# Twenty-three units of weights multiplied as plain fp32 in a two-block model of 2816- and 1280-wide layers

## The chip, the cores and the metric

One core of one Trainium2 chip runs the whole program in one launch. The metric is device time in microseconds from the first to the last instruction of the core; the median of the runs counts. Engines are named as in the profile: PE (TensorE) multiplies, PEld is its weight load, DVE is VectorE, ACT is ScalarE, POOL is GpSimd, SP is SyncE, whose queue issues the transfers of the weights.

## The reference

A block of two layers on 256 tokens of 1024 features, then a second block of two layers on those tokens and 16 meta tokens, 272 in all. Everything is float32.

```
x = layer_norm(ALPHA*x + 0.5*swiglu(x, w_in, w_out))          # 22 tiles of 128 wide
mix = (gelu(y_br) * rg_lru(conv(u_br), gate_w, ...)) @ w_out  # first layer: 1280 wide
mix = dilated_attention(x, k, v, w_q, w_o)                    # second layer
proj = h @ w_in                                               # second block, twice:
mix = concat(retention, pooling, forgetting attention) @ w_out
h = layer_norm_2(ALPHA*h + mix); h = layer_norm_2(ALPHA*h + (silu(h@w1) * (h@w3)) @ w2)
```

In `rg_lru` two gates are products of the convolved `u` with 256x256 blocks of `gate_w`, five blocks for each gate; from the gates come the factors of a scan along the tokens.

## The kernel before

**Tiling.** Activations stand with the features on the partitions: `xf[:, k, tokens]` is feature tile k of 8 in fp32. Every product of weights is a row of multiplies with a 128x128 weight tile as the stationary operand and 256 or 272 token columns as the moving one, summed over k in a PSUM bank.

**Splitting.** A number x is written as a high part (x rounded to fp32r) and a low part (x minus the high part). A weight tile is multiplied three times as fp32r (`mm3`): high by high, high by low, low by high. The activations are split into `gh` and `gl` by the norms, the convolved `u` into `uch` and `ucl`, the recurrent stage's output into `yh` and `yl`.

**Weights.** All weights come in one stream of 537 units of 8 tiles (128x1024, 512 KB), in the order in which PE uses them. `_dma` fetches unit u into one of 5 buffers `raw`, on SP's queue. `_hi` makes `whi` of it in two ACT casts of 128x512 (L87), `_lo` makes `wlo` in two subtractions (L99) on DVE, or on POOL while `lo_pool` is set. A buffer `raw` is free again when its `wlo` is made. `pump` runs ahead of PE by up to 6 units, and `w` hands out the tiles.

**Stages around the change.** `rg` is the recurrent stage, units 66 to 100. Its first 4 output tiles (`filler`) are multiplied before the norm is finished, the statistics of the norm lie amid them. Then: 4 tiles of `u` (units 70 to 73), gates 0 (74), 2 tiles of `u` (75, 76), gates 1 and 2 (77, 78), and gelu groups 0 to 4 of two units each with gates 3 and 4 between them (79 to 90). DVE makes the convolutions (L508, L510), the split of `uc` (L515, L516), the scans (L561) and the gelu's polynomial (L547, L548, L550); ACT makes tanh, exp and sqrt. At last `out_proj` multiplies `yh` and `yl` (units 91 to 100) in 8 output tiles, the first four together, so that the fifth pair of rows of `y` is wanted in unit 95. While `filler` is over and `out_proj` has not begun, `lo_pool` is set: POOL makes the low parts of the units that are split in that time.

`mixer(0)` is the first mixer of the second block, from unit 347: six tiles (`emb_filler`) before two norms are finished, then with 272 columns a group of two (`G`, units 353 and 354: keys of the retention with the forget logits, and values), pairs V_F (355, 356), K_R and Q_R (357, 358), Q_R and U_P (359, 360), and further pairs with the attention's heads between them. The logits go through some 20 small DVE instructions to `cs`, which SP's queue copies into `Kz`; the first head's scores need it between units 359 and 360.

**Order.** The instructions of an engine are run in their order, and each waits for what it needs. A tile framework sets the order from the code, the priorities (`high_priority` around the norms) and its own schedule.

Of the kernel before, what the change touches and what calls it, by code (L numbers as in the profile page):

```python
# [8 lines left out]
F32 = mybir.dt.float32  # L9
# [27 lines left out]
RAWS = 5  # L37
N_HEADS = 16
# [19 lines left out]
class Builder:  # L58
# [13 lines left out]
    # ---------------------------------------------------------------- weights  # L72
# [7 lines left out]
    def _hi(self):  # L80
        u = self.nhi
        while self.ndma < min(u + RAWS, N_UNIT):
            self._dma()
        self.nhi += 1
        hi = self.p_w.tile([128, UNIT * 128], F32R, tag="whi", name="whi")
        for q in range(0, UNIT * 128, 512):
            self.nc.scalar.copy(hi[:, q:q + 512], self.raws[u][:, q:q + 512])  # L87
        self.his[u] = hi

    def _lo(self, pool=False):  # L90
# [3 lines left out]
        self.nlo += 1  # L94
        lo = self.p_w.tile([128, UNIT * 128], F32R, tag="wlo", name="wlo")
# [6 lines left out]
    def pump(self, n, pool=False):  # L102
        """Splits up to n more units of weights, the high parts one unit ahead of the low parts."""
# [7 lines left out]
    def w(self, spec, n=1):  # L111
# [3 lines left out]
        if o == 0:  # L115
            self.his.pop(u - 1, None)
            self.los.pop(u - 1, None)
            if not self.hold:
                self.pump(2)
# [3 lines left out]
        if n == 1:  # L123
            self.plan.append(spec)
        else:
            self.plan.extend(spec)
        return self.his[u][:, o * 128:(o + n) * 128], self.los[u][:, o * 128:(o + n) * 128]

    # ---------------------------------------------------------------- helpers
    def bank(self, n=1, hold=None):  # L130
        """The next free psum bank (or aligned pair, or three in a row); a held one is skipped until it is let go."""
# [17 lines left out]
    def mm3(self, out, w, xh, xl, start, stop):  # L149
# [19 lines left out]
    # ---------------------------------------------------------------- layer norm  # L169
# [4 lines left out]
    def emb_begin(self):  # L174
        """The columns and the meta tokens that the norm of all tokens adds to the first block's last one."""
# [8 lines left out]
    def sums(self, m, N, off, sq, eng, eng2=None):  # L184
        """Running sums of x and x^2 over the feature tiles."""
# [17 lines left out]
    def fold_to(self, m, ln, N):  # L203
        """Factor and columns of the next stage's first input."""
# [13 lines left out]
    def prep(self, ms, ln, N, off, fold=True):  # L218
        """What the next norm needs of the feature tiles ms, which end together."""
# [24 lines left out]
    def scale_in(self, m, ln, N, off):  # L244
        """x <- x g, once the sums have what they need of it."""
# [9 lines left out]
    def stats(self, N, eps, tail=None, dst=None):  # L255
        """Mean and deviation of every token from the running sums; tail: the last tile's share comes on top."""
# [23 lines left out]
    def table(self, func, after):  # L280
        """Has ScalarE load the table set of func ahead of its use."""
        self.nc.scalar.activation(self.dummy, after, func)

    def norm(self, ln, N, off):
        """Normalises all feature tiles, software-pipelined over VectorE and ScalarE."""
# [17 lines left out]
    def norm_last(self, ln, N, off, i, eng, rstd, nm):  # L303
        """Normalises a feature tile that scale_in has been over."""
# [17 lines left out]
    def filler(self, specs, ln, N, off, eps, pool, tag="fv", bufs=2, when=(1, 3)):  # L322
        """First output tiles of a stage, from the not yet normalised input."""
# [16 lines left out]
    def emb_filler(self, specs, eps_in, eps, pool, tag):  # L340
        """The first output tiles of the second block, from the first block's last sums: two norms are still to come.
        The first one is of the tokens without the meta tokens, the second one of all."""
# [46 lines left out]
    def group(self, specs, N, kout=False, mid=None):  # L389
        """Output tiles in pairs from the normalised input; returns one [128, 2, N] psum view per pair.  # L390
        mid: what is emitted after the first half."""
# [6 lines left out]
        for i, (k, t) in enumerate(order):  # L398
# [3 lines left out]
            self.mm3(P[t // 2][:, t % 2, :], self.w(specs[t](k)), self.gh[:, k, 0:N], self.gl[:, k, 0:N], st, k == KD - 1)  # L402
# [5 lines left out]
    def out_proj(self, K, hh, hl, spec, coef, ln, N, off, fold, waves, korder=None, hooks={}):  # L408
        """x <- x + coef * (h @ W), in waves of output tiles; hooks: what is emitted amid the first wave."""
# [22 lines left out]
    # ---------------------------------------------------------------- feed forward  # L432
# [26 lines left out]
    # ---------------------------------------------------------------- RG-LRU  # L459
    def rg(self, ln_in, ln_out, eps):  # L460
        nc = self.nc
        N, off = SEQ, META
        with self.tc.tile_pool(name="rg", bufs=1) as p:
# [38 lines left out]
            uc, uch, ucl = {}, {}, {}  # L502

            def conv(n, src):
# [8 lines left out]
                uch[n] = p.tile([128, 2, N], F32R, tag="uch", name="uch", bufs=2)  # L513
                ucl[n] = p.tile([128, 2, N], F32R, tag="ucl", name="ucl", bufs=2)
                nc.vector.tensor_copy(uch[n], c)  # L515
                nc.vector.tensor_tensor(ucl[n], c, uch[n].bitcast(F32), op=ALU.subtract)  # L516

            def gates(n):
                P = []
                for g in range(2):  # L520
                    b = self.pair_bank(N)
                    for m in range(2):
                        for k in range(2):
                            self.mm3(b[:, m, :], self.w(("rg_gate_w", (0, g, n), k, m * 128)), uch[n][:, k], ucl[n][:, k],
                                     k == 0 and m == 0, k == 1)
# [14 lines left out]
            self.lo_pool = True  # L540
# [57 lines left out]
            self.lo_pool = False  # L598
# [3 lines left out]
    # ---------------------------------------------------------------- shared keys and values  # L602
# [34 lines left out]
    # ---------------------------------------------------------------- dilated attention  # L637
    def attn(self, ln_in, ln_out, eps):
        nc = self.nc
        N, off = SEQ, META  # L640
        with self.tc.tile_pool(name="attn", bufs=1) as p:
# [20 lines left out]
            def put(pr, g, src):  # L662
                """High part of a head's queries in its own half of the partitions, low part in the other one."""
# [70 lines left out]
            def step(n=1):  # L734
                """Head i's scores while the heads before it are a stage further each."""
# [37 lines left out]
    # ---------------------------------------------------------------- second block's mixer  # L773
# [668 lines left out]
```

## Time and profile before

| | |
|---|---|
| runs | 1810.32, 1812.07, 1812.13 us; median 1812.07 us |
| span of the profiled execution | 1813.3 us, its only own time that is known |
| mean granted PE clock | 0.970 |
| PE, DVE, ACT, POOL busy | 96%, 70%, 57%, 13% |
| weight splits | 1074 casts on ACT; 1032 subtractions on DVE, 42 on POOL |

A PE that is busy in these tables is one that has a multiply under way; multiplies overlap, so the distance between the starts of two neighbours tells what one costs, and the duration of one is longer than that. A plain fp32 multiply stands in the trace as two records, an fp32r one as one.

### The profile page before, as it was taken

The numbers are of one execution on the slowest core, as the hardware profiler recorded it, in microseconds if no ns is written. First come the engines' busy times: TensorE is split into PE (matmuls) and PEld (weight loads), VectorE is DVE, ScalarE is ACT, GpSimd is POOL, SyncE is SP. The second block draws the span as 40 slices with busy tenths as digits, with TensorE's granted clock in tenths as the row PEclk, the third lists the DMA queues.
The fourth block names the chain that finished last, engine by engine and source line by source line (L and its number), as shares of the span: only waits on it lengthen the run. The fifth ranks groups of instructions, "written<-read, shape, count | busy, mean of one in ns | idle before, by whom it ended". The sixth has DMA issues, their size and how long they took to land.

```text
span 1813.3 us, 34554 instructions
## 1 busy us (share of the span) xinstructions
PE 1741.0 (96%) x13558; PEld 1675.4 (92%) x13558; DVE 1272.0 (70%) x2399; ACT 1032.6 (57%) x2090; POOL 230.0 (13%) x266
## 2 busy tenths in 40 slices
PE   8999978999999999999999999799999999999997
PEld 8999977999999999977789999788999998899996
DVE  6666899966676666756668666897965569687653
ACT  6444666744465444644547445775744457575443
POOL 0001355000100001201120001320200030120001
PEclk9999988999999999968999999999999999999999
DMA  8555435565548555732225555433365554246550
GB/s 292 185 187 186 145 105 168 170 209 186 182 156 280 186 187 186 208 118 82 82 85 179 188 183 184 154 106 106 118 208 176 177 188 152 83 129 223 186 186 35
DMA packets 85372, 296.80 MB, mean 164 GB/s; under 512 B 10892, under 2 KB 14232, under 8 KB 84696
## 3 DMA queue, kind: packets, MB, share of 16 engines
q1 hardware_dynamic: 80216, 283.79, 47.1%
q0 software_dynamic: 1424, 7.38, 1.3%
q10 hardware_dynamic: 3568, 3.41, 0.6%
q8 instruction: 106, 1.74, 0.4%
q14 instruction: 58, 0.48, 0.1%
HBM read 290.24 MB, written 4.19 MB: 162 GB/s over the span
## 4 chain that ended last, share of the span: by engine, by line
PE 82%; DVE 11%; ACT 3%; issue 2%; DMA 1%; POOL 1%; DVEq 0%; SPq 0%; POOLq 0%; ACTq 0%
PE ps L147 81%; DVE wlo L99 3%; DMA KL<-kl 1%; PE ps L155 1%; ACT whi L87 1%; DVE uc L510 0%; DVE gl L300 0%; DVE T L561 0%; DVE xf L252 0%; POOL wlo L99 0%; DVE nt L291 0%; DVE gl L215 0%; POOL acc L193 0%; DVE rstd L277 0%; DMA raw<-in_wst_dram 0%
## 5 line engine op out<-in xcount | busy, mean ns | idle before, releaser
L87 ACT CAST whi<-raw 128x512 fp32r<-128x512 f32 x1074 | 615.5, 617 | 525.7 <-issue 311.0
L99 DVE TENSOR_TENSOR wlo<-raw,whi 128x512 fp32r<-128x512 f32 x1032 | 685.7, 701 | 321.5 <-ACT whi L87 319.6
L147 PE MATMUL ps<-gh,whi 128*128 128x256 f32 (+3 forms) x2864 | 829.0, 290 | 19.6 <-ACT gh L297 8.7
L147 PE MATMUL ps<-gl,whi 128*128 128x256 f32 (+3 forms) x2864 | 823.3, 288 | 1.0 <-DVE gl L300 1.0
L147 PE MATMUL ps<-gh,wlo 128*128 128x256 f32 (+3 forms) x2864 | 818.4, 286 | 0.0
L147 PEld LDWEIGHTS ps<-gh,whi 128*128 128x128 f32 x2864 | 549.3, 192 | 27.2 <-ACT gh L297 9.3
L147 PEld LDWEIGHTS ps<-gl,whi 128*128 128x128 f32 x2864 | 550.9, 192 | 5.9 <-issue 2.6
L147 PEld LDWEIGHTS ps<-gh,wlo 128*128 128x128 f32 x2864 | 551.1, 192 | 1.3 <-issue 0.7
L147 PE MATMUL ps<-hh,wlo 128*128 128x256 f32 (+1 forms) x1056 | 298.0, 282 | 0.0
L147 PE MATMUL ps<-hh,whi 128*128 128x256 f32 (+1 forms) x1056 | 297.9, 282 | 0.0
L147 PE MATMUL ps<-hl,whi 128*128 128x256 f32 (+1 forms) x1056 | 297.7, 282 | 0.0
L147 PEld LDWEIGHTS ps<-hl,whi 128*128 128x128 f32 x1056 | 199.0, 188 | 0.0
L147 PEld LDWEIGHTS ps<-hh,whi 128*128 128x128 f32 x1056 | 199.0, 188 | 0.0
L147 PEld LDWEIGHTS ps<-hh,wlo 128*128 128x128 f32 x1056 | 198.8, 188 | 0.0
L193 POOL TENSOR_TENSOR acc<-xf 128x256 f32<-128x256 f32 (+1 forms) x10 | 7.6, 759 | 1060.7 <-DVE xf L252 907.7
L443 DVE TENSOR_TENSOR th<-th,ps 128x512 f32<-128x512 f32 (+1 forms) x62 | 42.9, 691 | 54.3 <-PE ps L147 54.3
L193 POOL TENSOR_TENSOR acc<-acc,xf 128x256 f32<-128x256 f32 (+1 forms) x50 | 45.5, 910 | 192.3 <-DVE xf L252 177.3
L99 POOL TENSOR_TENSOR wlo<-raw,whi 128x512 fp32r<-128x512 f32 x42 | 63.3, 1536 | 46.2 <-ACT whi L87 46.2
L252 DVE SCALAR_TENSOR_TENSOR xf<-ps,xf 128x256 f32<-128x256 f32 (+1 forms) x80 | 32.9, 422 | 41.1 <-PE ps L147 40.9
L198 ACT ACTIVATE sq<-xf 128x256 f32<-128x256 f32 (+1 forms) x88 | 35.6, 410 | 44.6 <-DVE xf L252 36.8
L211 ACT ACTIVATE gh<-xf,prm 128x256 fp32r<-128x256 f32 (+1 forms) x64 | 32.1, 508 | 47.9 <-DVE xf L252 47.9
L215 DVE SCALAR_TENSOR_TENSOR gl<-xf,prm,gh 128x256 fp32r<-128x256 f32 (+1 forms) x64 | 44.5, 706 | 11.0 <-ACT gh L211 11.0
(330 smaller groups left out, 1927.8 us busy)
## 6 DMA issues: line engine op xcount, KB each, us to landing
raw<-in_wst_dram SPq DMA_DIRECT2D x537, 512.0 KB, 3.4
cst<-in_c_mix_dram POOLq DMA_DIRECT2D x2, 1138.0 KB, 5.5
KH<-kh POOLq DMA_DIRECT2D x4, 512.0 KB, 13.7
kh<-kh ACTq DMA_DIRECT2D x4, 256.0 KB, 4.8
kl<-kl ACTq DMA_DIRECT2D x4, 256.0 KB, 6.6
vsc<-kt ACTq DMA_DIRECT2D x4, 256.0 KB, 6.0
KL<-kl POOLq DMA_DIRECT2D x1, 1024.0 KB, 21.5
Vt<-vsc POOLq DMA_DIRECT2D x1, 1024.0 KB, 23.9
```

The costliest lines, as they stand in the source:

```text
L87: self.nc.scalar.copy(hi[:, q:q + 512], self.raws[u][:, q:q + 512])
L99: eng.tensor_tensor(lo[:, q:q + 512], r[:, q:q + 512], h[:, q:q + 512], op=ALU.subtract)
L147: self.nc.tensor.matmul(out, lhsT, rhs, start=start, stop=stop, skip_group_check=True)
L155: self.nc.tensor.matmul(out, in_, self.ident[0:n, 0:n], start=True, stop=True, is_transpose=True, skip_group_check=True)
L193: eng.tensor_tensor(a[:, 0, 0:N], x0, x, op=ALU.add)
L198: self.nc.scalar.activation(sq[:, 0:N], self.xf[:, m, off:off + N], AF.Square)
L211: return self.nc.scalar.activation(self.gh[:, m, c], self.xf[:, m, off:off + N], AF.Copy, scale=g)
L215: return self.nc.vector.scalar_tensor_tensor(self.gl[:, m, c], self.xf[:, m, off:off + N], g, self.gh[:, m, c].bitcast(F32), op0=ALU.mult, ...
L252: self.nc.vector.scalar_tensor_tensor(x, banks[m][:, 0:N], coef, x, op0=ALU.mult, op1=ALU.add)
L443: nc.vector.tensor_tensor(th, th, pu, op=ALU.mult)
```

## The change

`NATIVE` names 23 units by number: 74, 77, 78, 81 and 84 (the five pairs of gates), 79, 80, 82, 83 and 85 to 90 (the five gelu groups), and 353 to 360 in the first mixer. For these neither `_hi` nor `_lo` does anything; `w` hands out the `raw` tile itself, and `mm3` makes one plain fp32 multiply of it with the unsplit activation, `xf` or `uc`. Their `raw` buffer is let go when PE has begun the next unit. The convolved `u` is no longer split. `lo_pool` is no longer set. The rest of the diff takes out comments and is left out here.

```diff
+NATIVE = {74, 77, 78, 81, 84, 79, 80, 82, 83, *range(85, 91), *range(353, 361)}
...
         self.nhi += 1
+        if u in NATIVE:
+            return
         hi = self.p_w.tile([128, UNIT * 128], F32R, tag="whi", name="whi")
...
         self.nlo += 1
+        if u in NATIVE:
+            return
         lo = self.p_w.tile([128, UNIT * 128], F32R, tag="wlo", name="wlo")
...
             self.los.pop(u - 1, None)
+            if u - 1 in NATIVE:
+                self.raws.pop(u - 1)
...
+        if u in NATIVE:
+            return self.raws[u][:, o * 128:(o + n) * 128], None
         return self.his[u][:, o * 128:(o + n) * 128], self.los[u][:, o * 128:(o + n) * 128]
...
-    def mm3(self, out, w, xh, xl, start, stop):
+    def mm3(self, out, w, xh, xl, start, stop, x=None):
+        if w[1] is None:
+            self.mm(out, w[0], x, start, stop)
+            return
...
-            self.mm3(P[t // 2][:, t % 2, :], self.w(specs[t](k)), self.gh[:, k, 0:N], self.gl[:, k, 0:N], st, k == KD - 1)
+            self.mm3(P[t // 2][:, t % 2, :], self.w(specs[t](k)), self.gh[:, k, 0:N], self.gl[:, k, 0:N], st, k == KD - 1,
+                     self.xf[:, k, LTOT - N:])
...
-                uch[n] = p.tile([128, 2, N], F32R, tag="uch", name="uch", bufs=2)
-                ucl[n] = p.tile([128, 2, N], F32R, tag="ucl", name="ucl", bufs=2)
-                nc.vector.tensor_copy(uch[n], c)
-                nc.vector.tensor_tensor(ucl[n], c, uch[n].bitcast(F32), op=ALU.subtract)
...
-                            self.mm3(b[:, m, :], self.w(("rg_gate_w", (0, g, n), k, m * 128)), uch[n][:, k], ucl[n][:, k],
-                                     k == 0 and m == 0, k == 1)
+                            self.mm3(b[:, m, :], self.w(("rg_gate_w", (0, g, n), k, m * 128)), None, None,
+                                     k == 0 and m == 0, k == 1, uc[n][:, k])
...
-            self.lo_pool = True
...
-            self.lo_pool = False
```

Lines of the changed kernel stand a little lower: the multiply of L147 is L156 there, the subtraction of L99 is L104, the cast of L87 is L90.

PE in the recurrent stage, from the last multiplies before gates 1 to the first of `out_proj`, after the change:

```order
L156 MATMUL ps<-gl,whi 128x256
L156 MATMUL ps<-gh,wlo 128x256
L156 MATMUL ps<-uc,raw 128x256 x16
L156 MATMUL ps<-xf,raw 128x256 x16
L156 MATMUL ps<-uc,raw 128x256 x8
L156 MATMUL ps<-xf,raw 128x256 x16
L156 MATMUL ps<-uc,raw 128x256 x8
L156 MATMUL ps<-xf,raw 128x256 x48
L156 MATMUL ps<-yh,whi 128x256
```

Before, the same stretch held three multiplies for each of these 112, with `uch`, `ucl` or `gh`, `gl`; with the 8 of gates 0 it is 120 multiplies in place of 360.

DVE at the end of the recurrent stage before: from the fifth gelu group's first instruction (L547 here) to the fifth low part of `y`:

```order
L547 TENSOR_SCALAR gy<-gy 128x512
L99 TENSOR_TENSOR wlo<-raw,whi 128x512
L548 TENSOR_TENSOR gy<-gy,ps 128x512
L160 TENSOR_TENSOR yl<-gy,yh 128x512
L99 TENSOR_TENSOR wlo<-raw,whi 128x512 x2
L550 SCALAR_TENSOR_TENSOR gy<-gy,ps 128x512
L99 TENSOR_TENSOR wlo<-raw,whi 128x512
L566 TENSOR_TENSOR gy<-gy,T 128x512
L99 TENSOR_TENSOR wlo<-raw,whi 128x512 x2
L160 TENSOR_TENSOR yl<-gy,yh 128x512
```

and after (L555 is the first instruction there), with the subtraction that stands in front of it:

```order
L172 TENSOR_TENSOR yl<-gy,yh 128x512
L104 TENSOR_TENSOR wlo<-raw,whi 128x512
L555 TENSOR_SCALAR gy<-gy 128x512
L104 TENSOR_TENSOR wlo<-raw,whi 128x512
L556 TENSOR_TENSOR gy<-gy,ps 128x512
L104 TENSOR_TENSOR wlo<-raw,whi 128x512 x2
L558 SCALAR_TENSOR_TENSOR gy<-gy,ps 128x512
L104 TENSOR_TENSOR wlo<-raw,whi 128x512
L574 TENSOR_TENSOR gy<-gy,T 128x512
L104 TENSOR_TENSOR wlo<-raw,whi 128x512 x2
L172 TENSOR_TENSOR yl<-gy,yh 128x512
```

About as many subtractions lie amid the group as before, seven and seven up to its last `yl`. But those of units 91 to 95, ten in all, which POOL made before, now stand on DVE too: 16 subtractions of units 91 and on are ahead of that `yl` where 7 were, the first of them in the third group.

DVE in the first mixer's second norm (L273 to L292), before:

```order
L273 SCALAR_TENSOR_TENSOR var<-ps,var 128x272
L99 TENSOR_TENSOR wlo<-raw,whi 128x512
L274 TENSOR_SCALAR var<-var 128x272
L99 TENSOR_TENSOR wlo<-raw,whi 128x512 x2
L371 TENSOR_TENSOR fv<-ps,r_13228 128x544
L99 TENSOR_TENSOR wlo<-raw,whi 128x512
L277 RECIPROCAL rstd<-var 128x272
L371 TENSOR_TENSOR fv<-ps,r_13228 128x544
L278 SCALAR_TENSOR_TENSOR nm<-ps,rstd 128x272
```

and after:

```order
L285 SCALAR_TENSOR_TENSOR var<-ps,var 128x272
L286 TENSOR_SCALAR var<-var 128x272
L289 RECIPROCAL rstd<-var 128x272
L383 TENSOR_TENSOR fv<-ps,r_12878 128x544
L290 SCALAR_TENSOR_TENSOR nm<-ps,rstd 128x272
```

The four subtractions are gone from between the variance and the mean, and one of the two `fv` stands behind them now.

## Rows read from the trace of the kernel before

**Rows 1.** The page: the chain that ended last, share of the span by engine

```profile
PE 82%; DVE 11%; ACT 3%; issue 2%; DMA 1%; POOL 1%; DVEq 0%; SPq 0%; POOLq 0%; ACTq 0%
```

**Rows 2.** Busy time (count) by stretch: length, PE, PEld, DVE, ACT, POOL, clock, DMA, GB/s

```profile
1150.00:1270.00 120.00, 105.58 (x731) 95.47 (x730) 103.74 (x269) 83.85 (x205) 18.73 (x30) 0.94 0.33 107
...
207.50:302.00 94.50, 73.53 (x577) 71.81 (x576) 88.44 (x134) 61.81 (x123) 63.25 (x42) 0.92 0.36 119
```

**Rows 3.** What PE waited for in 195 to 335: total, times, longest

```profile
PE ps L147 <- DVE uch L515: 8.9, 1, 8.9
PE ps L147 <- DVE yl L160: 7.7, 2, 6.9
PE ps L147 <- ACT gh L297: 2.2, 1, 2.2
PE ps L147 <- DVE uc L510: 2.0, 1, 2.0
```

**Rows 4.** What PE waited for in 1143 to 1257

```profile
PE ps L147 <- ACT gh L297: 6.2, 1, 6.2
PE ps L147 <- DVE acc L193: 3.5, 1, 3.5
```

**Rows 5.** Busy time in stretches at the lower clock, columns as in Rows 2

```profile
231.60:241.90 10.30, 6.08 (x28) 6.11 (x29) 10.30 (x24) 1.65 (x4) 1.17 (x1) 0.50 0.26 88
296.50:306.70 10.20, 5.83 (x26) 5.71 (x27) 9.51 (x13) 5.26 (x11) 5.45 (x4) 0.50 0.55 172
1173.70:1180.50 6.80, 5.23 (x23) 5.23 (x24) 6.80 (x19) 5.78 (x12) 0.00 (x0) 0.50 0.24 77
1207.90:1211.30 3.40, 3.40 (x13) 3.04 (x14) 3.40 (x7) 0.59 (x2) 2.54 (x3) 0.51 0.71 202
```

**Rows 6.** POOL's groups in 195 to 335: busy us, mean ns | idle before

```profile
L99 POOL TENSOR_TENSOR wlo<-raw,whi 128x512 fp32r<-128x512 f32 x42 | 63.3, 1536 | 46.2 <-ACT whi L87 46.2
```

**Rows 7.** Lines 547, 548, 561 over the program: shortest, median, longest in ns

```profile
L547 DVE TENSOR_SCALAR gy<-gy x5: 419/1439/1582, 262.2 to 303.9; 128x512 f32<-128x512 f32 x5
...
L548 DVE TENSOR_TENSOR gy<-gy,ps x5: 672/677/689, 264.2 to 304.8; 128x512 f32<-128x512 f32 x5
...
L561 DVE TENSOR_TENSOR_SCAN T<-R,V x10: 659/1425/1786, 264.8 to 297.5; 128x256 f32<-128x256 f32 x10
```

**Rows 8.** PE in order of time, split weights, 256 columns: start, duration, what

```profile
134.27 0.28 PE L147 MATMUL ps<-gh,whi 128*128 128x256 f32 x1
...
135.93 0.28 PE L147 MATMUL ps<-hh,wlo 128*128 128x256 f32 x1
```

**Rows 9.** PE in order of time, 272 columns, split and then plain fp32

```profile
1251.70 0.29 PE L147 MATMUL ps<-gh,whi 128*128 128x272 f32 x1
...
1252.32 0.28 PE L147 MATMUL ps<-gh,wlo 128*128 128x272 f32 x1
1252.45 1.08 PE L147 MATMUL ps<-ua,pw 128*128 128x272 f32 x4
1253.36 0.38 PE L155 MATMUL ps<-ident,on 128*128 128x128 f32 x2
```

**Rows 10.** The page: the two halves of a split, and the transfer of a unit (us to landing)

```profile
L87 ACT CAST whi<-raw 128x512 fp32r<-128x512 f32 x1074 | 615.5, 617 | 525.7 <-issue 311.0
L99 DVE TENSOR_TENSOR wlo<-raw,whi 128x512 fp32r<-128x512 f32 x1032 | 685.7, 701 | 321.5 <-ACT whi L87 319.6
...
raw<-in_wst_dram SPq DMA_DIRECT2D x537, 512.0 KB, 3.4
```

**Rows 11.** DVE's groups in 207.5 to 302, columns as in Rows 6

```profile
L516 DVE TENSOR_TENSOR ucl<-uc,uch 128x512 fp32r<-128x512 f32 x5 | 5.1, 1013 | 0.0
...
L515 DVE CAST uch<-uc 128x512 fp32r<-128x512 f32 x5 | 3.6, 710 | 0.1
```

**Rows 12.** The chain of waits in the second norm: start, us, what

```profile
1167.52 1.20 DVE wlo L99 x2
...
1174.91 0.32 ACT gh L297
```

More of the change, by code (lines that the diff above doesn't have):

```diff
@@ L500, in wi @@
                 return lambda k: ("rg_w_in", (0,), k, c * 128)
-            uc, uch, ucl = {}, {}, {}
+            uc = {}
             def conv(n, src):
```

## The prediction

> **What bounds the kernel now.** I read the page's chain by engine first. PE carries 82% of it and DVE 11% [rows 1], so over the whole program PE's own multiplies set the time, and a change that makes PE cheaper or dearer shows at once. Then I read the busy times of the two stretches that the change touches [rows 2], and there the picture differs. In the recurrent stage PE is busy 73.5 of 94.5 us and DVE 88.4; in the first mixer PE 105.6 of 120 and DVE 103.7. DVE is nearly full in the first, and PE waits for it. The list of PE's waits names what ends them: the split of the convolved `u` (8.9 us in one piece, before gates 0), the low part of `y` before `out_proj` (7.7), `gh` (2.2), `uc` (2.0), together 20.8 us [rows 3]. In the mixer it is `gh` at the second norm (6.2) and `acc` at the statistics of the first (3.5) [rows 4].
>
> A wait has a second price. Two stretches of about 10 us in the recurrent stage run at a granted clock of 0.50, and in each PE is busy for only some 6 us [rows 5]: it stands idle for four, and then multiplies at the level of 1.2 GHz in place of 2.4. Half of the busy time is what the lower level costs: 6.08/2 + 5.83/2 = 5.9 us. In the mixer it is 5.23/2 + 3.40/2 = 4.3.
>
> Why is DVE so full? POOL makes 42 subtractions there, 63.3 us of work [rows 6]. In the same time DVE instructions that have only SBUF operands come in two lengths: L547 takes 419 ns at the shortest and 1439 at the median, the scan L561 659 and 1425, while L548, which reads PSUM, is 672 to 689 always [rows 7]. So I read POOL's subtractions as what stretches DVE's.
>
> The Trainium skill, page "GPSIMD Engine Reference", has a table by which GpSimd's SBUF interfaces are shared with VectorE, with contention for DVE instructions that have two SBUF inputs or run in a two-port mode. The trace agrees, with L547 and L548 as its two sides. By that rule the stretch ends when POOL stops.
>
> **The change part by part.**
>
> *Three multiplies become one, 184 times.* Fifteen units in the recurrent stage are 15 x 8 = 120 weight tiles with 256 columns, eight units in the mixer are 64 tiles with 272. The cost of an fp32r multiply is the distance between starts: at 256 columns 14 steps in 135.93 - 134.27 = 1.66 us [rows 8], 0.118 each, three of them 0.354. At 272 it is 6 steps in 1251.70 to 1252.45, 0.125 each, three 0.375. The plain fp32 multiply stands in the same rows: four records, so two multiplies, in 1253.36 - 1252.45 = 0.91 us, 0.455 each at 272 columns [rows 9], and scaled by columns 0.43 at 256 (an estimate). So a plain multiply is dearer than the three that it replaces, by 0.077 and 0.080: 120 x 0.077 = +9.2 us in the recurrent stage and 64 x 0.080 = +5.1 in the mixer, all on the path wherever PE does not wait. At the lower level it would be twice that.
>
> *The splits go.* 46 casts on ACT, 46 x 0.617 = 28.4 us [rows 10]; `uch` and `ucl`, 3.6 + 5.1 = 8.7 us on DVE [rows 11]; POOL's 42 subtractions. Units 75, 76 and 91 to 95 keep their low parts, 14 subtractions, which go to DVE; two of unit 74 leave it. That is 12 x 0.701 = +8.4 us for DVE [rows 10], as much as the split of `u` gives back. DVE's net in the recurrent stage is then the stretch. By median against shortest it is (1425 - 659) x 10 = 7.7 us for the scans and (1439 - 419) x 5 = 5.1 for L547 [rows 7]; if DVE's other instructions on SBUF operands behave alike, perhaps 20 in all (an estimate). None of these is on the path itself; what counts is the waits of [rows 3].
>
> The wait for `uch` (8.9): the instruction waited for is gone, gates 0 now wait for `uc` itself. Late next is the norm's tail on DVE, then the four-instruction convolution. DVE has 1.7 us less to do per pair of tiles and works unstretched. I leave 1.5 for it and the old wait for `uc` together (2.0 before), and bound it by 0 and 8.9. The wait for `gh` (2.2) falls to 0.5, since ACT has no casts in front of the norm there.
>
> The wait for `yl` (7.7): the fifth gelu group's polynomial and scan come sooner, unstretched, and PE comes later by most of the 9.2. Against it, the DVE rows show sixteen subtractions of units 91 and on ahead of the last `yl`, where seven were. Each waits for its cast, the cast for its transfer, and the transfer for a buffer that a plain unit now holds until PE has begun the next. Unit 95's buffer comes free when PE is through unit 90, a transfer takes 3.4 us to landing [rows 10], and two casts and subtractions follow. PE wants it in the fifth unit of `out_proj`, four units of 8 x 0.354 = 2.83 us after its start, 11.3 us. So it lands in time by itself, but what is queued behind a subtraction that waits on DVE is the polynomial and `yl`. I leave 3.0 us here; the ends are 0 and 7.7.
>
> Waits in the recurrent stage: 20.8 - (0.5 + 1.5 + 3.0) = 15.8 us gone. Of the clock's 5.9 I take 3.7 as gone with them, since one of its two stretches is the wait for `uch` and the other the wait for `yl`, and the second stays in part. The stage: +9.2 - 15.8 - 3.7 = -10.3 us; the ends are +9.2 with no gain, and 9.2 - 20.8 - 5.9 = -17.5.
>
> *The mixer.* In the second norm four subtractions leave the chain of DVE; two of them take 1.20 us, so all four 2.4, and PE's start hung on `gh` 0.32 later, which plain multiplies do not need as they read `xf` [rows 12]. ACT loses 16 casts of 0.617 around it. I take 4.0 off the wait of 6.2, between 2.4 + 0.3 and 6.2. Of the wait for `acc`, 3.5 us, I take 3.1, since casts and subtractions of units 353 to 356 stood amid the statistics; between 0 and 3.5. Of the clock's 4.3 I take 1.7, the part of the second stretch, and leave the first, as a norm with PE idle remains. The stage: +5.1 - 4.0 - 3.1 - 1.7 = -3.7; the ends are +5.1 - 2.7 = +2.4 and 5.1 - 9.7 - 4.3 = -8.9.
>
> One cover must hold. SP's queue is moved past more raw transfers that wait for PE, and the copy of `cs` into `Kz` stands behind them; scores of the first head want it. I cost this at nothing: it stands after the transfer that waits for unit 358, and two units, 7.3 us at 0.455 a tile, lie before the scores. If the cover fails, it is a transfer of 3.4 us.
>
> *The sum.* -10.3 - 3.7 = -14.0 us against the profiled execution's span of 1813.3, 1799.3. The median of the runs is 1812.07, 1.2 below that span; so the forecast is **1798**. With the ends for single waits that may well fall otherwise (3 us at `yl`, 2 at the clock, 2 in the mixer, either way) its own range is 1790 to 1804.
>
> **The rivals.**
>
> *Held buffers.* The subtractions of 91 to 98 wait for late buffers and hold DVE, so that the wait of 7.7 for `yl` and its half-clock stretch of 2.9 stay: 4.7 + 2.2 = 6.9 later, 1805. For it: sixteen subtractions ahead of `yl`, and only 5 buffers. Against: a plain unit takes PE 3.44 us, as long as a transfer, so buffers come free at the rate at which they fill.
>
> *All waits go.* Both stages at their far ends: -17.5 - 8.9 = -26.4, 1786. For it: DVE loses some 20 us of stretch against waits of 20.8. Against: norms keep a chain of several engines, on which PE must wait.
>
> *Four full passes.* If the plain multiply costs four fp32r distances, 0.472 and 0.500, its extra is 120 x 0.118 + 64 x 0.125 = 22.2 us in place of 14.3: 7.9 later, 1806. Against: 0.455 was measured at 272 columns [rows 9]; for it: that was a run of two multiplies only.
>
> The Trainium skill, page "FP8 and Floating Point Precision", section "TensorE Precision Notes", says that true FP32 is four passes through the array; taken with the distances of the fp32r multiplies, that is this rival. The trace shows 0.455 where the rule so read gives 0.500.
>
> *Slower: the chain keeps its length.* If DVE's long instructions are not POOL's doing, PE's longer multiplies and DVE's chain, which follow on each other, simply add. Then only the split of `u` (1.7 us a pair) leaves the wait for `uch`, and 2.7 the mixer's: +9.2 - 1.7 + 5.1 - 2.7 = +9.9, 1822. It decides once the waits and the lower clock together give back less than 14.3 us of the 26.7 + 14.0 listed in [rows 3, 4, 5]. For it: the long and the short instructions were read from one execution. Against: the PSUM readers, which do not stretch.
>
> That the change would not do what it says is excluded by the order: 120 multiplies stand in place of 360.
>
> **How the numbers follow.** Forecast 54%, all waits gone 20%, held buffers 15%, four passes 4%, slower 7%. 1784 to 1806 leaves out the slower case and a few per cent beyond the far ends. A measurement tells a difference of 0.2%, some 3.6 us, from none. Faster by that: 54 + 20 + most of the 15 and the 4, 89%. Within: the late edges of those and the early edge of the last, 5%. Slower: 6%.
>
> **What would show it.** Right: PE's waits in 195 to 335 down from 20.8 to about 5, with the one before gates 0 under 2; L547 and L561 all near their shortest; no half-clock stretch around the gates; plain multiplies 0.43 us apart at 256 columns, 0.455 at 272. Held buffers: DVE idle for ACT's casts amid the fourth and fifth gelu groups, and a wait of 7 us for `yl`. The prediction is wrong if the long DVE instructions remain with POOL idle, if plain multiplies stand 0.47 apart, or if the Kz transfer becomes a wait of PE.

## The result, and the profile after

The changed kernel takes 1789.16 us (median of 4 runs, 1786.91 to 1792.91) against 1811.19 of the kernel before; ratio 0.9891, 95% interval 0.9870 to 0.9913. The forecast was 1798: its direction was right, but the gain of 22 us is half as much again as the 14 forecast. The time lies 0.8 us below the forecast's own range (1790 to 1804), inside the wider one of 1784 to 1806, and nearer to the rival in which all waits go (1786).

The chain that ended last now hangs on DVE for 7% of the span, where it was 11% [rows 1]:

```profile
PE 86%; DVE 7%; ACT 2%; DMA 2%; issue 1%; POOL 1%; SPq 0%; DVEq 0%; POOLq 0%; ACTq 0%
```

A stage is measured here from the first multiply of its first unit to the first multiply of the next stage. By stretches, columns as in [rows 2], the four rows are the recurrent stage, its `out_proj` alone, the attention and the first mixer of the changed kernel:

```profile
196.70:307.10 110.40, 110.14 (x724) 103.05 (x723) 97.00 (x219) 76.40 (x149) 0.00 (x0) 1.00 0.48 163
278.60:307.10 28.50, 28.50 (x242) 28.48 (x241) 26.58 (x55) 20.97 (x42) 0.00 (x0) 1.00 0.72 247
729.60:923.50 193.90, 188.71 (x1076) 151.32 (x1075) 134.72 (x314) 104.29 (x226) 35.42 (x50) 0.91 0.35 109
1116.00:1254.80 138.80, 127.19 (x817) 112.54 (x816) 113.70 (x282) 89.91 (x218) 34.61 (x49) 0.98 0.34 118
```

The kernel before has these rows for the recurrent stage, the attention and the mixer:

```profile
197.10:328.00 130.90, 108.72 (x844) 106.00 (x843) 124.11 (x217) 89.82 (x178) 63.27 (x42) 0.92 0.41 136
750.60:950.60 200.00, 195.80 (x1076) 157.15 (x1076) 134.76 (x314) 104.69 (x226) 35.84 (x50) 0.87 0.34 106
1143.30:1282.90 139.60, 125.16 (x881) 114.35 (x880) 122.03 (x298) 97.63 (x234) 34.50 (x49) 0.95 0.35 117
```

The reader is to see three things. The recurrent stage is 20.5 us shorter; PE is busy in all but 0.3 us of it, at a granted clock of 1.00, and DVE has 27.1 us less to do although it took over 12 subtractions net. The mixer is 0.8 shorter. The attention, whose code is the same in both, is 6.1 shorter, with its clock at 0.91 in place of 0.87. The profiled spans differ by 27.5 us (1813.3 to 1785.8), and these three make 27.4; whether the attention's part belongs to the change has to be tested.

In the recurrent stage no wait of PE is left: the view of waits in 195 to 305 has no row, where it had the 20.8 us of [rows 3]. DVE's instructions on SBUF operands are back at their shortest, to compare with [rows 7]; the first row is the former line 547, the second the scan:

```profile
L555 DVE TENSOR_SCALAR gy<-gy x5: 400/417/426, 245.7 to 281.4; 128x512 f32<-128x512 f32 x5
...
L569 DVE TENSOR_TENSOR_SCAN T<-R,V x10: 665/684/691, 244.6 to 268.6; 128x256 f32<-128x256 f32 x10
```

PE in order of time (start, duration, what, records) shows the price of a plain multiply in two records:

```profile
244.23 3.62 PE L156 MATMUL ps<-uc,raw 128*128 128x256 f32 x16
247.69 7.07 PE L156 MATMUL ps<-xf,raw 128*128 128x256 f32 x32
254.59 3.62 PE L156 MATMUL ps<-uc,raw 128*128 128x256 f32 x16
```

From start to start 8 multiplies take 3.46 us and 16 take 6.90: 0.432 each, as estimated from 272 columns [rows 9].

In the mixer, PE's wait for `gh` of 6.2 us [rows 4] has become one of 1.6 for `xf`. The wait for `acc` has not fallen, and one for `P` has grown from 1.0 to 3.8 (total, times, longest):

```profile
PE ps L167 <- DVE P L928: 3.8, 1, 3.8
PE ps L156 <- DVE acc L205: 3.6, 1, 3.6
PE ps L167 <- DVE fv L383: 1.8, 1, 1.8
PE ps L156 <- ACT xf L306: 1.6, 1, 1.6
```

### The profile page after: what moved, and what is told of

Read it like the earlier page. It is cut to its first block, busy times and chain, and to the rows that moved or that the text cites. A ratio compares the mean times of both kernels' runs of the same rounds, so it can differ in the third digit from the quotient of the medians.

```text
span 1785.8 us, 34026 instructions
## 1 busy us (share of the span) xinstructions
PE 1737.0 (97%) x13374; PEld 1663.8 (93%) x13374; DVE 1236.9 (69%) x2385; ACT 1010.0 (57%) x2044; POOL 166.7 (9%) x224
## 4 chain that ended last, share of the span: by engine, by line
PE 86%; DVE 7%; ACT 2%; DMA 2%; issue 1%; POOL 1%; SPq 0%; DVEq 0%; POOLq 0%; ACTq 0%
PE ps L156 85%; DVE wlo L104 2%; DMA KL<-kl 1%; PE ps L167 1%; ACT whi L90 1%; DVE xf L264 0%; DVE gl L227 0%; POOL acc L205 0%; DVE nt L303 0%; DMA raw<-in_wst_dram 0%; DVE nt L304 0%; DVE cp L859 0%; DVE xf L322 0%; DVE rx L997 0%; DVE xf L323 0%
## 5 line engine op out<-in xcount | busy, mean ns | idle before, releaser
L104 DVE TENSOR_TENSOR wlo<-raw,whi 128x512 fp32r<-128x512 f32 x1028 | 683.0, 700 | 323.2 <-ACT whi L90 321.5
L90 ACT CAST whi<-raw 128x512 fp32r<-128x512 f32 x1028 | 589.6, 617 | 529.1 <-issue 309.5
L156 PE MATMUL ps<-gh,whi 128*128 128x256 f32 (+4 forms) x2720 | 785.3, 289 | 8.3 <-ACT whi L90 7.0
L156 PE MATMUL ps<-gl,whi 128*128 128x256 f32 (+4 forms) x2720 | 778.1, 286 | 0.2
L156 PE MATMUL ps<-gh,wlo 128*128 128x256 f32 (+4 forms) x2720 | 774.5, 285 | 0.0
L156 PEld LDWEIGHTS ps<-gh,whi 128*128 128x128 f32 x2720 | 519.8, 191 | 15.5 <-ACT whi L90 9.0
L156 PEld LDWEIGHTS ps<-gl,whi 128*128 128x128 f32 x2720 | 520.8, 191 | 4.2 <-issue 2.4
L156 PEld LDWEIGHTS ps<-gh,wlo 128*128 128x128 f32 x2720 | 521.1, 192 | 0.7 <-issue 0.6
L156 PE MATMUL ps<-hh,wlo 128*128 128x256 f32 (+1 forms) x1056 | 298.0, 282 | 0.0
L156 PE MATMUL ps<-hh,whi 128*128 128x256 f32 (+1 forms) x1056 | 297.9, 282 | 0.0
L156 PE MATMUL ps<-hl,whi 128*128 128x256 f32 (+1 forms) x1056 | 297.7, 282 | 0.0
L156 PEld LDWEIGHTS ps<-hl,whi 128*128 128x128 f32 x1056 | 199.0, 188 | 0.0
L156 PEld LDWEIGHTS ps<-hh,whi 128*128 128x128 f32 x1056 | 199.0, 188 | 0.0
L156 PEld LDWEIGHTS ps<-hh,wlo 128*128 128x128 f32 x1056 | 198.8, 188 | 0.0
L156 PE MATMUL ps<-xf,raw 128*128 128x256 f32 (+1 forms) x288 | 65.1, 385 | 1.6 <-ACT xf L306 1.6
L156 PEld LDWEIGHTS ps<-xf,raw 128*128 128x128 f32 x288 | 54.5, 190 | 10.9 <-ACT xf L306 2.0
L210 ACT ACTIVATE sq<-xf 128x256 f32<-128x256 f32 (+1 forms) x88 | 35.6, 410 | 46.2 <-DVE xf L264 37.5
```

The lines of the kernel that those rows point to most:

```text
L104: eng.tensor_tensor(lo[:, q:q + 512], r[:, q:q + 512], h[:, q:q + 512], op=ALU.subtract)
L156: self.nc.tensor.matmul(out, lhsT, rhs, start=start, stop=stop, skip_group_check=True)
L210: self.nc.scalar.activation(sq[:, 0:N], self.xf[:, m, off:off + N], AF.Square)
```

## The experiments

The theory after the comparison: POOL's 42 subtractions stretched DVE, and the split of `u` held the gates; both went. The rival: what counts is the number of casts and subtractions, and POOL's part is none. A second rival, that PE waited for low parts which POOL made late, has 0.2 us to show in the kernel before, in 195 to 335:

```profile
PE ps L147 <- POOL wlo L99: 0.2, 1, 0.2
```

Lengths of stages are in us, from one profile of each kernel. The recurrent stage repeats where its code does: 110.4 in all three kernels with its 15 units plain and POOL idle, 130.1 to 130.9 in the three with the code of before. The shared keys and values together with the feed-forward stage behind them take 233.9 to 234.3 in every kernel. So differences of a microsecond can be read there; the attention and the mixer scatter by more.

| kernel | POOL's subtractions | plain units, recurrent stage | recurrent stage | with the stage behind it | mixer | attention |
|---|---|---|---|---|---|---|
| before | 42 | 0 | 130.9 | 319.4 | 139.6 | 200.0 |
| changed | 0 | 15 | 110.4 | 298.9 | 138.8 | 193.9 |
| rg_only | 0 | 15 | 110.4 | 299.0 | 139.7 | 198.6 |
| mix_only | 42 | 0 | 130.1 | 318.6 | 137.2 | 194.1 |
| pool_off | 0 | 0 | 121.0 | 309.3 | 140.5 | 197.2 |
| pool_busy | 42, idle work | 15 | 152.9 | 341.4 | 135.9 | 192.2 |
| ffn_16 | 42 | 0 | 130.7 | 329.4 | 139.6 | 199.6 |
| pool_keep | 14 | 15 | 116.3 | 304.8 | 139.9 | 199.4 |
| fewer | 0 | 11 | 109.8 | 298.9 | 137.2 | 202.9 |
| attn | 0 | 15 | 110.4 | 299.0 | 139.7 | 202.5 |
| gates_only | 0 | 5 gates | 108.1 | 298.0 | 139.8 | 199.6 |
| gelu_only | 0 | 10 gelu | 116.5 | 305.5 | 136.8 | 193.7 |
| nine | 0 | 9 | 108.8 | 298.7 | 136.7 | 199.4 |
| gates_pool | 34 | 5 gates | 122.9 | 311.4 | 135.9 | 190.2 |

**The two halves.** `rg_only`: `NATIVE` without `range(353, 361)`. `mix_only`: `NATIVE = {*range(353, 361)}`, with `uch`, `ucl` and `lo_pool` as before.

> Only the 15 units of the recurrent stage are plain fp32; the mixer splits its units as before. By the traces of before and after the recurrent stage gave 20.4 us, the mixer 0.8 and the attention, which the change does not touch, 6.2. Theory A (the recurrent stage is nearly all of it, and the mixer's plain units give as much as they cost): 1789 to 1791 us, within 2 us of the full change. Theory B (the mixer is worth the 3.7 us of the forecast): 1793. No wait of PE in the recurrent stage, its clock 1.00.

> Only the 8 units of the mixer are plain fp32; the recurrent stage and its use of POOL are as before. Theory A: within 2 us of before (1809 to 1812), with PE's wait for gh in the second norm gone and a new wait for P or fv in its place. Theory B: 3.7 us faster, 1807.5. The attention has the code of before: if its length is again some 6 us off the one before, the 6.2 us are scatter between executions; if it is as in the profile of before, they belong to the change.

Measured: 1792.71 us, ratio 0.9895 (0.9868 to 0.9922), and 1802.23, ratio 0.9976 (0.9958 to 0.9995). The time of `rg_only` lies between the two theories' figures and that of `mix_only` is lower than either's; the total cannot tell them apart, for the attention has moved again. In `mix_only`, up to the mixer the code of before, it is 194.1; in `rg_only`, the code of the changed kernel, 198.6:

```profile
728.70:927.30 198.60, 194.35 (x1077) 156.36 (x1076) 134.68 (x314) 104.48 (x226) 35.81 (x50) 0.88 0.34 106
```

```profile
748.40:942.50 194.10, 189.91 (x1077) 151.69 (x1076) 134.91 (x314) 104.51 (x226) 35.16 (x50) 0.90 0.35 109
```

So the attention's length goes with the clock that it is granted, whichever code runs in front of it. Over the 13 kernels in which its code is the same it takes 190.2 to 202.9 us, with 27.3 to 54.6 us of it at the lower clock, 0.4 to 0.5 us for each. The 6.1 us of the comparison are scatter of this kind. The total scatters alike with the code fixed: six executions of `rg_only` took 1781.93 to 1793.66 us.

The mixer itself: with plain units 135.9 to 139.9 in nine kernels, mean 137.6; with split ones 139.6 to 140.5 in five, mean 139.8. The plain units win 2.2 us there, where the forecast had 3.7. The two largest waits of `mix_only` are also in the changed kernel, but the wait for `P` is 1.6 here and 1.5 to 1.8 in the other plain mixers, so its 3.8 was not a fixed cost:

```profile
PE ps L156 <- DVE acc L205: 3.7, 1, 3.7
PE ps L156 <- ACT xf L306: 1.9, 1, 1.9
PE ps L167 <- DVE fv L383: 1.8, 1, 1.8
PE ps L167 <- DVE P L934: 1.6, 1, 1.6
```

The spread of the nine has a second cause in the traces. In `gates_only` and `pool_keep`, the two longest plain mixers (139.8, 139.9), PE waits 6.4 us for `acc` where the others have 3.6 to 4.1. There one of POOL's sums takes 6.25 us, while DVE runs its instructions of 0.4 us without a gap, none of them stretched; in the changed kernel the same sum takes 0.79:

```profile
1129.28 6.25 POOL L205 TENSOR_TENSOR acc<-xf 128x272 f32<-128x272 f32 x1 [2.18 <-DVE xf L323]
```

```profile
1124.91 0.79 POOL L205 TENSOR_TENSOR acc<-xf 128x272 f32<-128x272 f32 x1 [2.18 <-DVE xf L323]
```

So the two engines hold each other up, and it can be POOL that loses; what decides it is not shown. The other six without the long wait for `P` take 135.9 to 137.2, mean 136.6, which is 3.2 less than the split ones.

**POOL alone.** `pool_off` is the kernel before in which `lo_pool` is never set:

```diff
-            self.lo_pool = True
...
-            self.lo_pool = False
```

> The kernel before with lo_pool never set: no plain multiplies, and DVE makes the 42 subtractions that POOL made. Theory A (POOL's subtractions stretch DVE's instructions on SBUF operands): L547's place and the scans go to 0.42 and 0.68 us, DVE loses some 30 us of stretch and gains 42 x 0.70 = 29 us, and the time is 1806 to 1818. Theory B (the long instructions are not POOL's doing): they stay long, DVE has 29 us more in a stage that it bounds, and the time is 1830 or more.

Measured: 1795.77 us, ratio 0.9923 (0.9898 to 0.9949). Not one weight is plain here, DVE makes all low parts itself, and the recurrent stage is 9.9 us shorter. The rival, 1830 or more, is out. Theory A was right on DVE's durations and too low on the gain, as the time is below its 1806 to 1818:

```profile
L559 DVE TENSOR_SCALAR gy<-gy x5: 422/422/428, 259.7 to 292.0; 128x512 f32<-128x512 f32 x5
...
L573 DVE TENSOR_TENSOR_SCAN T<-R,V x10: 665/676/687, 253.7 to 296.0; 128x256 f32<-128x256 f32 x10
```

```profile
197.20:318.20 121.00, 110.50 (x844) 108.03 (x844) 116.34 (x257) 90.78 (x179) 0.00 (x0) 0.93 0.44 140
```

DVE is busy for 116.3 us with 40 instructions more, where it was 124.1 before. The 42 subtractions that took POOL 63.3 us cost DVE less than they had cost it on POOL. PE's longest waits here are for the split of `u` and for a cast:

```profile
PE ps L156 <- DVE uch L528: 4.5, 2, 2.8
PE ps L156 <- ACT whi L90: 2.4, 1, 2.4
PE ps L156 <- DVE ucl L529: 1.1, 2, 0.6
```

**POOL's traffic by itself.** `pool_busy` is the changed kernel with work on POOL whose results nobody reads:

```diff
+            nc.gpsimd.memset(da, 0.0)
+            nc.gpsimd.memset(db, 1.0)
+            for _ in range(42):
+                dc = p.tile([128, 512], F32, tag="dc", name="dc", bufs=2)
+                nc.gpsimd.tensor_tensor(dc, da, db, op=ALU.subtract)
```

> The changed kernel, with 42 subtractions of 128x512 on POOL at the start of the recurrent stage whose operands are constants in SBUF and whose results nobody reads. Theory A (it is POOL's traffic that stretches DVE): the median of the gelu's first DVE instruction or of the scans rises again above 1 us while POOL is busy, PE waits for DVE once more, and the time is 1794 to 1806. Theory B (the gain comes from the casts and subtractions that are gone, and POOL's traffic does not matter): DVE's durations stay at 0.42 and 0.68, and the time is 1787 to 1791.

Measured: 1828.41 us, ratio 1.0106 (1.0077 to 1.0135): slower than the kernel before, and 42 us longer in the recurrent stage than the changed kernel. The direction is theory A's, the size far beyond it, and the gelu and the scans, for which it expected more than 1 us, start later and stay short (the scans at 679 ns). The 42 run back to back from the stage's start, 198.3 to 259.7, and fall on the norm. The stage, POOL's group, DVE's groups in 197 to 262 of this kernel for the split of the norm and its product (busy, mean ns), and PE's waits:

```profile
196.90:349.80 152.90, 120.83 (x725) 111.13 (x724) 138.68 (x219) 76.37 (x149) 62.42 (x44) 0.88 0.36 117
```

```profile
L556 POOL TENSOR_TENSOR dc<-da,db 128x512 f32<-128x512 f32 x42 | 61.4, 1500 | 0.1
```

```profile
L312 DVE TENSOR_TENSOR gl<-xf,gh 128x256 fp32r<-128x256 f32 x8 | 9.1, 1143 | 0.0
L304 DVE TENSOR_TENSOR nt<-nt,nm 128x256 f32<-128x256 f32 x8 | 7.6, 953 | 0.0
...
L329 DVE TENSOR_TENSOR fv<-ps,rstd 128x512 f32<-128x512 f32 x2 | 1.4, 678 | 0.0
```

```profile
PE ps L156 <- ACT gh L309: 15.3, 1, 15.3
PE ps L156 <- DVE gl L312: 12.8, 6, 4.2
```

In the changed kernel the same two are 416 and 419 ns:

```profile
L304 DVE TENSOR_TENSOR nt<-nt,nm 128x256 f32<-128x256 f32 x8 | 3.3, 419 | 0.0
...
L312 DVE TENSOR_TENSOR gl<-xf,gh 128x256 fp32r<-128x256 f32 x8 | 3.3, 416 | 0.0
```

The row of L329, which reads PSUM, stays at 678. There is no data dependence between POOL's idle work and DVE's, so the stretch is shown to come from POOL's work. That it is the traffic on SBUF is the reading of the rows that do and do not stretch.

The means hide two lengths. In order of time, DVE's instructions beside POOL's of 1.5 us:

```profile
221.00 0.41 DVE L303 TENSOR_TENSOR nt<-xf,rstd 128x256 f32<-128x256 f32 x1
221.34 1.22 DVE L505 SCALAR_TENSOR_TENSOR e<-e,z 128x10 f32<-128x10 f32 x1
...
237.36 1.48 DVE L312 TENSOR_TENSOR gl<-xf,gh 128x256 fp32r<-128x256 f32 x1
238.77 1.49 DVE L303 TENSOR_TENSOR nt<-xf,rstd 128x256 f32<-128x256 f32 x1
```

An instruction is not stretched in proportion to its size. Here DVE gets through one such instruction of 1.5 us, or a pair of 0.4 and 1.2, in the time of each of POOL's. L505 has 10 columns and takes 0.17 us in the changed kernel. Of the 41.7 us by which DVE's busy time is longer than in the changed kernel, 19.4 are on the 25 instructions of 10 or 20 columns and 16.4 on the norm's 28 (L303, L304, L312, L331). PE pays for it with 31.8 us more of idle time and 10.7 more of busy time, at a granted clock of 0.88, together the 42.5 of the stage.

**Some of POOL's work.** `pool_keep` is the changed kernel with `lo_pool` set where it was, 14 subtractions.

> The changed kernel with lo_pool set as before, so that POOL makes the 14 subtractions of units 75, 76 and 91 to 95. Theory A (POOL's traffic stretches DVE, here a third of what it was): the recurrent stage, 110.5 us in the changed kernel, takes 112 to 118, with waits for DVE; the time 1791 to 1797. Theory B (what counts is how many subtractions DVE has): DVE is 10 us freer, the stage takes 110 or less, the time 1785 to 1789.

Measured: 1794.21 us, ratio 0.9935 (0.9912 to 0.9958), and the stage takes 116.3 us, with a wait of 2.8 for `gh`. This is theory A's: 14 subtractions on POOL cost 5.9 us.

**The price of plain units.** `ffn_16` is the kernel before with `NATIVE = {*range(110, 126)}`.

> The kernel before with 16 other units plain fp32: 110 to 125, in the middle of a feed-forward stage in which PE never waits and whose length (first multiply of unit 101 to the first of the next stage) is 188.5 us. Theory A (a plain multiply costs 0.432 where three split ones cost 0.354, and nothing is to be won where no wait is): 128 x 0.078 = 10.0 us longer, 198.5, the time about 1820. Theory B (the plain multiply itself is what made the changed kernel faster, or costs nothing as it needs fewer weight loads): 188 or less, the time 1810 or less.

Measured: 1817.8 us, ratio 1.0066 (1.0040 to 1.0092). The feed-forward stage in the kernel before, and in this one:

```profile
328.00:516.50 188.50, 188.50 (x1588) 187.82 (x1587) 128.11 (x218) 104.48 (x202) 10.29 (x12) 1.00 0.57 188
```

```profile
327.50:526.20 198.70, 198.70 (x1460) 191.40 (x1459) 109.39 (x186) 88.53 (x170) 10.26 (x12) 1.00 0.56 179
```

10.2 us for 128 tiles, 0.080 each, against 0.078 expected. DVE is 18.7 us less busy and it wins nothing, as PE waits for nothing there.

**Which units of the recurrent stage.** `fewer` splits units 87 to 90 again, `nine` 85 to 90, `gates_only` all ten gelu units; `gelu_only` splits the gates' five, with `uch` and `ucl`; `gates_pool` is `gates_only` with `lo_pool` set.

> The changed kernel with units 87 to 90 (the last two gelu groups) split again: PE saves 32 x 0.078 = 2.5 us, DVE makes 8 subtractions more, 5.6 us, ACT 8 casts. Theory A (DVE and ACT have slack in the stage by now): the stage falls from 110.5 to 108, the time by 2.5. Theory B (the chain to the last yl has none): PE waits for yl before out_proj and the stage takes 111 to 115.

> The changed kernel with six gelu units (85 to 90) split again, nine plain in the recurrent stage. PE saves 48 x 0.078 = 3.7 us, DVE makes 12 subtractions more, 8.4 us. With four split again PE saved 2.5 and the stage 0.6. Theory A (slack is left): the stage 107 to 109, the best of all. Theory B (the low parts for out_proj and the last yl are late): 110 to 113 with a wait for yl.

> The changed kernel with the ten gelu units (79, 80, 82, 83, 85 to 90) split again; the gates' five and the mixer's eight stay plain, POOL makes no low parts. The recurrent stage took 121.0 us with POOL off and no plain unit, 110.4 with all 15. Theory A (the remaining 10.6 come from the split of u in front of the gates): 111 to 114, though DVE has 20 subtractions more. Theory B (they come from the gelu's casts and subtractions): 117 to 121.

> The other half: the ten gelu units and the mixer's eight plain, the gates' units split with uch and ucl as before, POOL makes no low parts. Theory A: waits of PE for uch as with POOL off, the recurrent stage 116 to 121. Theory B: 111 to 114, and the wait for uch mostly gone.

> As the kernel with only the gates' five units (and the mixer's eight) plain, but POOL makes the low parts of the ten gelu units, of 75 and 76 and of 91 to 95: 34 subtractions. Theory A (both are needed: without the split of u the gates start early, but POOL's traffic stretches the norm, the scans and the polynomials): the recurrent stage 118 to 126 us, against 108.1 with POOL off. Theory B (the split of u was what mattered, and DVE is better off with 34 subtractions less): 104 to 110.

Measured: `fewer` 1785.86, ratio 0.9884 (0.9856 to 0.9912); `nine` 1782.23, 0.9841 (0.9814 to 0.9869); `gates_only` 1789.08, 0.9862 (0.9827 to 0.9897); the other two have one run each, 1788.46 and 1791.13, and are read by their stages alone. In `fewer` the stage gave 0.6 of the 2.5 us, with a wait for `yl` of 1.4, and the next stage gave that back: between the theories, and no gain. In `nine` the stage is 108.8, theory A, but 298.7 with the stage behind it, the same as with 15 plain units. With the gates alone it is 298.0: the ten gelu units bring 0.9 us of loss together with the stage behind. `gates_only` beats both of its theories, 108.1 against 111 to 114 and 117 to 121; `gelu_only` is at theory A's lower end, 116.5, with the wait for `uch` there. First the stage of `gates_only`, then the waits of `gelu_only`:

```profile
196.00:304.10 108.10, 104.84 (x804) 101.15 (x803) 105.77 (x236) 84.73 (x168) 0.00 (x0) 1.00 0.49 159
```

```profile
PE ps L156 <- DVE uch L528: 5.7, 2, 4.0
PE ps L156 <- DVE ucl L529: 0.9, 2, 0.4
```

In `gates_only` PE is busy for 5.3 us less than in the changed kernel and DVE for 8.8 more, 105.8 of 108.1. PE waits again, 2.2 for `uc`, but for less than the multiplies save.

With gates split or plain, POOL on or off, the stage takes 130.9 and 122.9 with POOL, 121.0 and 108.1 without. Plain gates alone win 8.0, POOL off alone 9.9, both 22.8, 4.9 more than the sum. `gates_pool` is theory A's: PE no longer waits for `uch`, but DVE's scans are at 1076 ns on average and PE waits 7.9 before `out_proj`:

```profile
L570 DVE TENSOR_TENSOR_SCAN T<-R,V 128x256 f32<-128x256 f32 x10 | 10.5, 1076 | 0.0
```

```profile
PE ps L156 <- ACT yh L171: 7.9, 2, 6.9
```

No kernel of these is shown to beat the changed one. `nine` has the lowest ratio, and its interval ends where that of the changed kernel begins (0.9869, 0.9870); but its stages in the table differ from the changed kernel's by 0.2 in the recurrent part and 2.1 in a mixer of the same code.

**The attention's lower clock.** `attn`: `NATIVE` of the recurrent stage and `range(253, 273)`, the mixer split.

> The changed kernel with the mixer split again and the 20 units 253 to 272 of the attention's queries plain fp32. In the attention PE waits hardly at all, but it runs at the lower clock for 37 to 54 us in the traces so far. Theory A (PE bounds it, the lower clock does not depend on the form of the multiply): 160 x 0.078 = 12.5 us longer, 205 to 212 from the first multiply of unit 249 to the next stage, the time about 1802. Theory B (a denser PE stays at the higher clock, worth up to 19 to 27 us there): the stage 185 to 195, the time 1775 to 1788.

Measured: 1792.12, ratio 0.9915 (0.9887 to 0.9943). The stage:

```profile
728.90:931.40 202.50, 202.38 (x916) 152.56 (x915) 110.06 (x275) 85.33 (x188) 32.17 (x50) 0.91 0.34 106
```

The stage takes 202.5 us, in neither theory's range, with 37.5 of them at the lower clock. Kernels with split queries and 37.5 us there (`mix_only`, `gelu_only`) took 194.1 and 193.7, so the plain units cost some 8.6. PE's busy time has the full price: 202.4 against 189.9 us in both, 12.5 more. The rest is PE's idle time, which theory A left out: 4.2 and 3.8 us there, 0.1 here. Theory B's saving is not there, as the lower clock lasts longer than in the shortest split runs (27.3 and 34.1).

## Why the prediction was right, and where it was short

*The price of plain multiplies* was right: 0.432 and 0.458 measured (the latter the median distance of the mixer's plain multiplies at full clock), 0.43 and 0.455 forecast; +9.2 us in the recurrent stage stands. By the four-pass rival it would have been 0.472 and 0.500; it is out. The ratio to the fp32r distance is 3.66 at either width. The Trainium skill, "FP8 and Floating Point Precision", section "TensorE Precision Notes", with its four passes is not refuted by it: what fell is to price a pass at the distance of an fp32r multiply. No run here shows what a pass takes.

*POOL's work as the cause of DVE's long instructions* was right, and it is shown by `pool_off` and `pool_busy` rather than argued. Its size was not: the prediction put the stretch at "perhaps 20" us, and DVE's busy time fell by 27.1, while the split of `u` (8.7) and the 12 subtractions more (8.4) nearly cancel. The Trainium skill, "GPSIMD Engine Reference", section "1. Specifications", says that instructions of VectorE with two SBUF inputs or in a two-port mode contend with GpSimd; the durations of L304 and L312 with POOL busy agree, 953 and 1143 ns for 419 and 416.

*The residual waits* were the step that failed: "I leave 3.0 us here" for `yl`, "1.5" for `uc`, 0.5 for `gh`, and 2.2 us of the lower clock. All were nothing. The recurrent stage gave 20.5 and not 10.3: 5.0 us of waits, 2.2 of clock, 1.4 of waits under a microsecond that [rows 3] leaves out. The last 1.6 are about what nine stops of PE cost beside their idle time, an estimate from [rows 8]: 0.28 - 0.12 = 0.16 us of overlap lost at each, 1.4 in all. The sixteen subtractions ahead of the last `yl` did not matter in the changed kernel. Where more stand in DVE's order, a short wait for `yl` returns: 0.8 us in `gates_only`, with ten gelu units split again, and 1.4 in `fewer`, with four. I counted what stands in DVE's order ahead of that `yl`, and did not carry the shorter instructions of the whole stage through to it: DVE's busy time fell from 124.1 to 97.0 us.

*The mixer* was over-sized, 3.7 for 0.8 in the pair compared, 2.2 on the mean of the nine plain ones and 3.2 in the six without the long waits for `P` and for POOL's sum. The second norm's wait fell by 4.6 against 4.0; the wait for `acc`, of which I took 3.1, did not move:

```profile
1163.98 0.82 PE L147 MATMUL ps<-acc,ones 128*128 128x272 f32 x1 [3.52 <-DVE acc L193]
```

```profile
1134.40 0.50 PE L156 MATMUL ps<-acc,ones 128*128 128x272 f32 x1 [3.64 <-DVE acc L205]
```

From the stage's start (1143.3, 1116.0) that is 20.7 and then 18.4 us, so DVE's chain did become 2.3 shorter, as the prediction had it. But PE's order changed as well: these statistics stand behind 107 multiplies of the stage in all nine plain mixers and behind 126 in all five split ones, so PE comes to them sooner and waits as long. The two waits are one chain with PE's work between them. Together they fell from 9.7 to 5.2, 4.5 where the prediction took 4.0 and 3.1 separately. The waits for `fv` and `P` rose from 1.2 and 1.2 to 1.8 and 3.8, and one of 1.9 for `rx` went.

*The queue of SP*, costed at nothing, was nearly right: the copy into `Kz` ends a wait of 0.3 us. By the prediction's own words that is a sign of being wrong, but it is a tenth of the transfer of 3.4.

*The forecast's sum*, -14.0, was short by 10.2 in the recurrent stage and long by 1.5 in the mixer, by its mean; 20.5 and 2.2 together are 22.7, against the 22.0 of the medians. The attention's scatter lay outside the argument; from its shortest to its longest it is 12.7 us, nearly the gain that was forecast.

## What to carry to other kernels

Where DVE's instructions of one line come in two lengths, look at what GpSimd does in the longer ones before you give it more to do: moving 42 subtractions back to DVE made DVE's own time shorter (124.1 to 116.3 us). Count the number of DVE's instructions beside GpSimd's and not their size, since one of 10 columns grew from 0.17 to 1.2 us. Plain fp32 in place of three fp32r multiplies costs PE 0.08 us a tile and pays only where the split stands on the path, which were five units of fifteen here. And compare stage by stage: the length of one stage that the change does not touch scattered by 12.7 us, with a gain of 22.

## What the runs showed of the hardware that was not expected

The two engines hold each other up by the instruction. Beside POOL's subtractions of 1.5 us, instructions of 10 columns and of 256 alike took up to 1.2 and 1.5 us on DVE (0.17 and 0.42 in the changed kernel), and beside DVE's unbroken run one sum of POOL took 6.25 us in place of 0.79. So 42 subtractions at the stage's start, with no consumer and beside many short instructions of DVE, cost 42.5 us. The 9.9 us for the 42 useful ones spread over the stage (130.9 to 121.0) and the 14.8 for 34 of them beside plain gates (122.9 to 108.1) are no measure of the same thing, as DVE was spared the same subtractions there.

The attention, busy on PE almost throughout, was at the lower clock for 27.3 to 54.6 us in executions of the same code. In each of the 13 kernels the first of these stretches, 10 to 14 us long, begins behind an idle PE, with 2.0 to 4.4 us of idle time just ahead of it. All the others have no idle time of PE just ahead of them. A row of the changed kernel that holds one of them and most of another:

```profile
790.00:820.00 30.00, 29.99 (x154) 23.56 (x154) 15.99 (x45) 12.91 (x28) 3.47 (x6) 0.87 0.16 54
```

In `attn`, where PE does not wait, the first stretch is 3.4 us long and the others make up for it. So idle time, as the profile counts it, does not explain most of the lower clock, and why it varies was not found.
